# A decoder step on one core: final norm row left unscaled, three operand splits put behind the last head group's post-processing on ScalarE

## The chip, the cores and the metric

The kernel runs on one core of a Trainium2 chip. The metric is the device time of one execution in microseconds (us). The core's engines run side by side, each through its own list of instructions in order: TensorE (PE: matmuls, which write PSUM), VectorE (DVE), ScalarE (ACT), GpSimd (POOL), and SyncE (SP), on whose queue this kernel puts all its transfers. An instruction waits on its engine until what it reads has been written and the buffer that it writes is free; what stands behind it on that engine waits too.

## The reference, cut to what matters

One layer of a hybrid decoder on 2048 prompt tokens and 8 x 8 new tokens: RMSNorm, one input projection, four heads of differential attention, a convolution branch, both gated and concatenated into m, an output projection, residual and a final RMSNorm.

```python
def mix_out(att, conv, g_att, g_conv, w_out):
    m = jnp.concatenate([att * jax.nn.silu(g_att), conv * jax.nn.silu(g_conv)], axis=-1)
    return m @ w_out
...
o = rmsnorm(o, subln_g) * (1.0 - lam_init)
...
yp = yp + mix_out(att, conv, g_att, g_conv, w_out[l])
...
y_prompt = rmsnorm(yp, final_norm_g)
```

`rmsnorm(x, g)` is `x * rsqrt(mean(x*x) + EPS) * g` over rows of D = 1024.

## The kernel before, in words

The first 690 us are the input projections and the convolution; they are not touched. Behind them comes prompt attention, in 13 groups (h, G): head h, 512 query rows G. The order of the groups is h = 0 to 3 with G = 1 to 3 (head 0 from G = 0), and then (1,0), (2,0), (3,0). So (3,3) is the last large group, and three small ones follow it. Each group has four blocks of 128 query rows and two score maps m; each pair (block, m) is a score tile row: PE fills score tiles `S` in PSUM (`s_mm`, two buffers of 1024 columns), DVE takes their row minimum and copies them to SBUF (`s_min`, `pS` or `pL`), ACT makes exponentials with row sums (`exp_row`), POOL two small numbers (`coef`), DVE combines the two maps (`combine`), PE transposes (`pt`), ACT copies the transposes (`at`), and PE multiplies them with the values into `O`.

A group ends with its post-processing: `post1` copies `O` to `osb` and squares it into `o2` on ACT; `post15` adds a small diagonal to `o2` on POOL; `post2` sums the squares over partitions on PE, and takes logarithm and exponential (`rs`) on ACT; POOL multiplies with the gate, and SP writes the result to the scratch `md`.

The output projection works in 8 chunks of 256 tokens, in the order `OC` (2, 3, 4, 5, 6, 7, 0, 1). `out_chunk` loads m from `md` into the one buffer `mf`, and `m_split` makes a rounded high part `mH` (ACT) and the rest `mL` (DVE), so that three matmuls per weight block give the product's precision. `out_tile` does two tiles of 128 tokens, each in two halves of 512 columns: 24 matmuls into `yps`, then DVE adds the residual (`y`), ACT squares with a row sum, POOL takes the power -0.5, DVE scales with the norm row `fnt`, and SP writes the rows out. The weights are split in the same way by `wo_load`; k = 0 and 1 go to buffers of their own, k = 2 to 7 to buffers of the long score rows as these come free. The raw weights (`wor`) lie in the buffers that `mH` and `mL` use later.

The first three chunks are traced at low priority beside the last groups: PE has one PSUM bank for them (pool psM) until attention is over, and three more after that. The small sample attention (`dec_stream`) is interleaved with later chunks.

Nothing orders the engines by hand. The instructions are traced in the program's order with priorities, and a scheduler with a timeline of its own then fixes each engine's list; the list is static, and each engine waits at its head. `tc.issue_after(ins)` makes the instructions traced in its block stand behind `ins` on `ins`'s engine.

Of the kernel before, what the change touches and what calls it, by code (L numbers as in the profile page):

```python
# [1 line left out]

# [9 lines left out]
AF = mybir.ActivationFunctionType  # L12
ALU = mybir.AluOpType
# [5 lines left out]
D = 1024  # L19
# [13 lines left out]
EPS = 1e-5  # L33
# [19 lines left out]
LOW = 3000  # L53
# [3 lines left out]
OC = (2, 3, 4, 5, 6, 7, 0, 1)  # L57
# [17 lines left out]
def hybrid_step(  # L75
# [6 lines left out]
    PE, DVE, ACT, POOL, SP = nc.tensor, nc.vector, nc.scalar, nc.gpsimd, nc.sync  # L82
# [397 lines left out]
    def post1(Gd):  # L480
        osb = op.tile([P, 512], F32, name="osb", tag="osb")
        ACT.activation(osb, Gd["O"], AF.Copy)
        o2 = op.tile([P, 512], F32, name="o2", tag="o2", bufs=1)
        ACT.activation(o2, osb, AF.Square)
        Gd["post"] = osb, o2

    def post15(Gd):
        o2 = Gd["post"][1].rearrange("p (b t) -> p b t", t=P)
# [9 lines left out]
    def post2(Gd):  # L498
        osb, o2 = Gd["post"]
        gate = Gd["gate"]  # L500
        pm = tps()
        PE.matmul(pm, lhsT=onesd, rhs=o2, start=True, stop=True)

        def ev():
            rs = op.tile([P, 512], F32, name="rs", tag="rs", bufs=1)
            ACT.activation(rs, pm, AF.Ln)
            ACT.activation(rs, rs, AF.Exp, scale=-0.5)
            POOL.tensor_tensor(out=osb, in0=osb, in1=gate, op=ALU.mult)
            POOL.tensor_tensor(out=gate, in0=osb, in1=rs, op=ALU.mult)
            SP.dma_start(md[Gd["G"]][:, Gd["h"], :], gate)  # L510
        evac(ev)
# [82 lines left out]
    def tps(side=False):  # L594
        while len(pend) >= TB - 1:
            pend.pop(0)()
        if side:
            return PS["m"].tile([P, 512], F32, name="pt", tag="mt", bufs=PS["n"])
        return psT.tile([P, 512], F32, name="pt", tag="t", bufs=TB)

    def evac(fn):
        pend.append(fn)
# [119 lines left out]
    dk = {}  # L722
# [141 lines left out]
    for n, (h, G) in enumerate(groups):  # L864
        Gd = {"h": h, "G": G, "n": n}
# [34 lines left out]
    def end_unit(U, k):  # L900
        Gd = U["G"]
        h, G = Gd["h"], Gd["G"]
        ts_ = slice(G * 512, (G + 1) * 512)
        first = [U["s"] == 0]
        for fn in pv_items(U):
            def run(fn=fn):
                if first[0]:
                    first[0] = False
                    if (h, G) == (H - 1, 3):
                        pxs.clear()  # L910
                        out_open()
                    Gd["gate"] = op.tile([P, 512], F32, name="gate", tag="gate")
                    SP.dma_start(Gd["gate"], gd[h][:, ts_])
                    Gd["O"] = psO.tile([P, 512], F32, name="O", tag="O")
                U["O"], U["vt"] = Gd["O"], Gd["vt"]
                fn()
                flush()
            queue.append((k + D2, run))
        if U["s"] == 1:
            def p1():  # L920
                if (h, G) == (H - 1, 3):
                    for k in range(2):
                        wo_load(k)
                post1(Gd)
                post15(Gd)
                if h == 0 and G == 3:
                    flags["h0"] = True

            def p2():
                post2(Gd)  # L930
                flush()
                if (h, G) == (H - 1, 3):
                    for k in range(2, KC):
                        wo_load(k)
                    for c in OC[0:NE]:
                        side(out_chunk(c), off=-LOW)
                flags["wide"] = flags.get("wide") and (h, G) != (H - 1, 3)
            queue.append((k + D2, p1))
            queue.append((k + D3, p2))
# [15 lines left out]
    def out_open():  # L955
        nonlocal oy
        px_ctx.close()
        oy = ctx.enter_context(tc.tile_pool(name="oy", bufs=2, side="right", reuse_waits="tile"))
        dk["fnt"] = oy.tile([P, D], F32, name="fnt", tag="fnt", bufs=1)
        SP.dma_start(dk["fnt"], fng.to_broadcast([P, D]))  # L960
        POOL.tensor_scalar(out=dk["fnt"], in0=dk["fnt"], scalar1=float(D) ** 0.5, scalar2=None, op0=ALU.mult)
        for k in range(0, KC, 2):
            r = oy.tile([P, 2, D], F32, name="wor", tag="mH" if k % 4 == 0 else "mL")
            SP.dma_start(r, wout[k * P:(k + 2) * P, :].rearrange("(x p) d -> p x d", p=P))
            wor[k], wor[k + 1] = r[:, 0, :], r[:, 1, :]

    def out_tile(mH, mL, sl, xsrc, dst, nr, last=False):
        y = oy.tile([P, D], F32, name="y", tag="y")
        SP.dma_start(y[0:nr, :], xsrc)
        ss = oy.tile([P, 2], F32, name="yss", tag="yss")  # L970
        for hf in range(2):
            cs = slice(hf * 512, (hf + 1) * 512)
            yb.append(yb.pop(0))
            ps = yb[-1].tile([P, 512], F32, name="yps", tag="mt" if yb[-1] is psM else "y",
                             bufs=1 if yb[-1] is psM else 5 - DM)
            i = 0
            for k in (2, 3, 4, 5, 6, 7, 0, 1):
                for m, x in ((mH, 0), (mL, 0), (mH, 1)):
                    PE.matmul(ps, lhsT=m[:, k, sl], rhs=wo[k][x][:, cs], start=(i == 0), stop=(i == 3 * KC - 1))  # L979
                    i += 1  # L980
            yield
            DVE.tensor_tensor(out=y[0:nr, cs], in0=ps[0:nr, :], in1=y[0:nr, cs], op=ALU.add)  # L982
            jk = oy.tile([P, 512], mybir.dt.bfloat16, name="yjunk", tag="yjunk", bufs=1)
            ACT.activation(jk[0:nr, :], y[0:nr, cs], AF.Square, accum_out=ss[0:nr, hf:hf + 1])
        r = oy.tile([P, 1], F32, name="yr", tag="yr")
        POOL.tensor_scalar(out=r[0:nr, :], in0=ss[0:nr, 0:1], scalar1=ss[0:nr, 1:2], scalar2=D * EPS, op0=ALU.add,
                           op1=ALU.add)
        POOL.tensor_tensor(out=r[0:nr, :], in0=r[0:nr, :], in1=mhalf[0:nr, :], op=ALU.pow)
        for cs in (slice(0, 512), slice(512, D)) if last else (slice(0, D),):
            DVE.scalar_tensor_tensor(out=y[0:nr, cs], in0=y[0:nr, cs], scalar=r[0:nr, :], in1=dk["fnt"][0:nr, cs],  # L990
                                     op0=ALU.mult, op1=ALU.mult)
            SP.dma_start(dst[:, cs], y[0:nr, cs])

    def m_split(mf, n):
        mH = oy.tile([P, KC, 256], F32R, name="mH", tag="mH")
        mL = oy.tile([P, KC, 256], F32R, name="mL", tag="mL")
        ACT.activation(mH[:, :, 0:n], mf[:, :, 0:n], AF.Copy)
        DVE.tensor_tensor(out=mL[:, :, 0:n], in0=mf[:, :, 0:n], in1=mH[:, :, 0:n].bitcast(F32), op=ALU.subtract)
        return mH, mL

    def out_chunk(c, pre=None):
        mf = oy.tile([P, KC, 256], F32, name="mf", tag="mf", bufs=1)
        SP.dma_start(mf, md[c // 2][:, :, c % 2 * 256:c % 2 * 256 + 256])
        mH, mL = m_split(mf, 256)
        sm = pre() if pre else None
        for j in range(2):
            t = 2 * c + j
            yield from out_tile(mH, mL, slice(j * P, (j + 1) * P), xp[t * P:(t + 1) * P, :], yp[t * P:(t + 1) * P, :], P,
                                last=pre is not None and j == 1)
            if sm and j == 0:  # L1010
                yield from out_tile(*sm, slice(0, P), xs, ys, SMP)

    def wo_load(k):
        if k < 2:
            hi, lo = (pp.tile([P, D], F32R, name=f"wo{x}{k}", tag="wo", bufs=4) for x in range(2))
        else:
            tg = "pL1" if k < 4 else "pL0"
            w = pp.tile([P, 2, D], F32R, name=f"wo{k}", tag=tg, bufs=PBUFS[tg])
            hi, lo = w[:, 0, :], w[:, 1, :]
        r = wor[k]  # L1020
        ACT.activation(hi, r, AF.Copy, scale=gsub if k < 4 else 1.0)
        if k < 4:
            DVE.scalar_tensor_tensor(out=lo, in0=r, scalar=gsub, in1=raw(hi), op0=ALU.mult, op1=ALU.subtract)
        else:
            DVE.tensor_tensor(out=lo, in0=r, in1=raw(hi), op=ALU.subtract)
        wo[k] = hi, lo
# [3 lines left out]
    def side(gen, n=10 ** 6, off=0):  # L1030
        with tc.high_priority(offset=off):
            for _ in gen:
                flush()
                n -= 1
                if n <= 0:
                    return False
        return True
# [127 lines left out]
```

## Time and profile before

| what | us |
|---|---|
| median of three runs (lowest, highest) | 1346.87 (1342.31, 1347.28) |
| the profiled execution: its time | 1346.68 |
| its span | 1344.8 |
| mean granted TensorE clock | 0.993 of full |
| matmuls of the output projection | 816, on PE from 1069.7 to 1337.4 |
| PE busy | 1287.8 of the span |

Times within the trace count from the span's start. A matmul's duration includes its pipeline, so that consecutive ones overlap; the distance of their starts is what PE is occupied. In brackets at a row's end stand the idle time of the engine before the instruction, and what ended it.

### The profile page before, as it was taken

The numbers are of one execution on the slowest core, as the hardware profiler recorded it, in microseconds if no ns is written. First come the engines' busy times: TensorE is split into PE (matmuls) and PEld (weight loads), VectorE is DVE, ScalarE is ACT, GpSimd is POOL, SyncE is SP. The second block draws the span as 40 slices with busy tenths as digits, with TensorE's granted clock in tenths as the row PEclk, the third lists the DMA queues.
The fourth block names the chain that finished last, engine by engine and source line by source line (L and its number), as shares of the span: only waits on it lengthen the run. The fifth ranks groups of instructions, "written<-read, shape, count | busy, mean of one in ns | idle before, by whom it ended". The sixth has DMA issues, their size and how long they took to land.

```text
span 1344.8 us, 19974 instructions
## 1 busy us (share of the span) xinstructions
PE 1287.8 (96%) x7552; PEld 1102.4 (82%) x7552; DVE 863.1 (64%) x1215; ACT 516.8 (38%) x949; POOL 249.5 (19%) x353
## 2 busy tenths in 40 slices
PE   6999999999999999999988999999999899999997
PEld 5898998998888888888866888888777677767776
DVE  7623998998999992333127777787778864214332
ACT  6622211211211222323236666656676864212221
POOL 3200200200201100000014233222324345301110
PEclk9999999999999999999989999999999999999999
DMA  8641330330432435333266455454264745558631
GB/s 270 201 132 50 82 119 33 105 112 24 128 112 60 146 141 167 134 119 111 80 139 171 134 152 141 115 150 115 50 147 117 238 111 163 193 189 277 243 126 63
DMA packets 127794, 180.23 MB, mean 134 GB/s; under 512 B 25170, under 2 KB 74578, under 8 KB 127698
## 3 DMA queue, kind: packets, MB, share of 16 engines
q1 hardware_dynamic: 127698, 178.96, 43.9%
q8 instruction: 59, 0.97, 0.3%
q14 instruction: 37, 0.30, 0.1%
HBM read 113.88 MB, written 65.04 MB: 133 GB/s over the span
## 4 chain that ended last, share of the span: by engine, by line
PE 78%; DMA 9%; DVE 4%; ACT 3%; issue 2%; POOL 1%; SPq 1%; DVEq 0%; POOLq 0%; ACTq 0%
PE zps L204 38%; PE yps L979 12%; PE zps L328 7%; PE O L696 6%; PE pt L551 3%; PE S L616 3%; PE pt L678 3%; PE S L617 3%; DMA kt<-kd 2%; DVE pL L661 1%; DMA wr<-in_wz 1%; DVE pL L638 1%; DMA qt<-qd 1%; DMA mf<-md 1%; DMA c<-cd 1%
## 5 line engine op out<-in xcount | busy, mean ns | idle before, releaser
L204 PE MATMUL zps<-hH,wH 128*128 128x512 f32 (+2 forms) x984 | 343.4, 349 | 3.0 <-ACT wH L160 3.0
L204 PE MATMUL zps<-hL,wH 128*128 128x512 f32 (+2 forms) x984 | 343.3, 349 | 0.0
L204 PE MATMUL zps<-hH,wL 128*128 128x512 f32 (+2 forms) x984 | 343.2, 349 | 0.0
L241 DVE SCALAR_TENSOR_TENSOR acc<-u,cst,acc 128x1024 f32<-128x1024 f32 x240 | 313.2, 1333 | 6.9 <-ACT acc L239 4.1
L204 PEld LDWEIGHTS zps<-hH,wH 128*128 128x128 f32 x984 | 185.0, 188 | 25.3 <-ACT wH L160 3.7
L204 PEld LDWEIGHTS zps<-hH,wL 128*128 128x128 f32 x984 | 185.2, 188 | 21.5
L204 PEld LDWEIGHTS zps<-hL,wH 128*128 128x128 f32 x984 | 185.1, 188 | 21.4
L979 PE MATMUL yps<-wo,mH 128*128 128x512 f32 x544 | 176.8, 401 | 0.8 <-DVE y L982 0.8
L616 PE MATMUL S<-kt,qt 128*128 128x512 f32 (+3 forms) x320 | 131.4, 414 | 18.9 <-DMA kt<-kd 4.9
L696 PE MATMUL O<-at,vt 128*128 128x256 f32 (+1 forms) x576 | 141.5, 373 | 1.8 <-ACT at L683 1.6
L979 PEld LDWEIGHTS yps<-wo,mH 128*128 128x128 f32 x544 | 101.7, 188 | 28.2 <-issue 3.2
L649 ACT ACTIVATE pL<-pL,mn 128x1152 f32<-128x1152 f32 (+7 forms) x64 | 104.3, 1630 | 40.9 <-DVE mn L641 40.6
L617 PE MATMUL S<-kt,qt 128*128 128x512 f32 (+3 forms) x320 | 114.9, 369 | 0.0
L696 PEld LDWEIGHTS O<-at,vt 128*128 128x128 f32 x576 | 102.4, 193 | 13.4 <-ACT at L683 2.8
L979 PE MATMUL yps<-wo,mL 128*128 128x512 f32 x272 | 108.7, 400 | 0.0
L683 ACT ACTIVATE at<-pt 128x512 f32<-128x512 f32 (+1 forms) x144 | 79.2, 567 | 55.3 <-PE pt L678 53.9
L638 DVE TENSOR_SCALAR_CACHE_REDUCE pL<-S 128x1024 f32<-128x1024 f32 x64 | 78.1, 1221 | 26.1 <-PE S L617 25.5
L616 PEld LDWEIGHTS S<-kt,qt 128*128 128x128 f32 x320 | 61.3, 192 | 39.0 <-issue 9.6
L661 DVE SCALAR_TENSOR_TENSOR pL<-pL,cf,pL 128x512 f32<-128x512 f32 (+2 forms) x112 | 80.7, 778 | 13.1 <-POOL cf L656 13.0
L641 DVE CUSTOM_DVE_ANT_0 pS<-S,trim 128x768 f32<-128x768 f32 (+7 forms) x64 | 47.2, 754 | 61.8 <-PE S L617 58.7
L982 DVE TENSOR_TENSOR y<-yps,y 128x512 f32<-128x512 f32 (+1 forms) x34 | 23.2, 689 | 90.1 <-PE yps L979 65.8
L655 POOL TENSOR_TENSOR cf<-sm,mone 128x1 f32<-128x1 f32 x64 | 40.2, 628 | 204.8 <-ACT pL L649 110.5
(163 smaller groups left out, 1947.4 us busy)
## 6 DMA issues: line engine op xcount, KB each, us to landing
qt<-qd SPq DMA_DIRECT2D x32, 512.0 KB, 7.2
wr<-in_wz SPq DMA_DIRECT2D x48, 256.0 KB, 3.5
kt<-kd SPq DMA_DIRECT2D x38, 256.0 KB, 5.1
xt<-in_xp SPq DMA_DIRECT2D x16, 512.0 KB, 5.2
mf<-md SPq DMA_DIRECT2D x8, 1024.0 KB, 7.1
y<-in_xp SPq DMA_DIRECT2D x16, 512.0 KB, 3.9
kr<-in_ck SPq DMA_DIRECT2D x32, 256.0 KB, 4.5
vr<-in_cv SPq DMA_DIRECT2D x32, 256.0 KB, 5.4
```

The lines of the kernel that those rows point to most:

```text
L204: PE.matmul(ps[:, 0:n], lhsT=wt[:, ks], rhs=ht[g][:, k, off:off + n], start=(i == 0), stop=(i == 3 * KC - 1))
L241: DVE.scalar_tensor_tensor(out=a, in0=u[:, t:t + HS], scalar=dwwt[:, cg, t:t + 1], in1=a, op0=ALU.mult, op1=ALU.add)
L328: PE.matmul(ps[0:n, 0:256], lhsT=ht[g][:, k, off:off + n], rhs=wt[:, sl], start=(i == 0), stop=(i == 3 * KC - 1))
L616: PE.matmul(ps[:, o:o + n], lhsT=t["mq"][:, m, qs_], rhs=kk, start=True, stop=False)
L617: PE.matmul(ps[:, o:o + n], lhsT=t["mq"][:, 2 + m, qs_], rhs=kk, start=False, stop=True)
L638: DVE.tensor_scalar(out=dst, in0=ps, scalar1=0.0, scalar2=None, op0=ALU.add, op1=ALU.min, accum_out=mn[:, m, 0:1])
L641: DVE.tensor_tensor_reduce(out=dst, in0=ps[:, 0:w], in1=trim[:, 1024 - w:] if diag else trim[:, 0:1].to_broadcast([P, w]), scale=1.0, scal ...
L649: ACT.activation(q, q, AF.Exp, bias=B["mn"][:, m, c:c + 1], scale=-1.0, accum_out=B["sm"][:, m, B["i"] % 4:B["i"] % 4 + 1])
L661: DVE.scalar_tensor_tensor(out=p0, in0=p1, scalar=B["cf"], in1=p0, op0=ALU.mult, op1=ALU.add)
L683: ACT.activation(at[:, 0:n * P], pt[:, 0:n * P], AF.Copy)
L696: PE.matmul(O[:, dst], lhsT=vt[j // 4][:, j % 4, :], rhs=at[:, src], start=(j == 0), stop=part)
L979: PE.matmul(ps, lhsT=m[:, k, sl], rhs=wo[k][x][:, cs], start=(i == 0), stop=(i == 3 * KC - 1))
```

## The change

Three things. The norm row `fnt` is no longer multiplied with the square root of 1024 on POOL; instead the Square of `out_tile` takes a scale of 1024 to the -0.5, and the constant added to the sum is EPS instead of 1024 EPS. The splits of weights k = 0 and 1, which were traced ahead of the post-processing of group (3,3), are traced behind its Square and must stand behind it on ACT. The split `mH` of the first chunk must stand behind that group's exponential on ACT.

```diff
@@ post1
-        ACT.activation(o2, osb, AF.Square)
+        ins = ACT.activation(o2, osb, AF.Square)
         Gd["post"] = osb, o2
+        return ins
@@ post2
-            ACT.activation(rs, rs, AF.Exp, scale=-0.5)
+            Gd["ri"] = ACT.activation(rs, rs, AF.Exp, scale=-0.5)
@@ end_unit
             def p1():
+                ins = post1(Gd)
                 if (h, G) == (H - 1, 3):
-                    for k in range(2):
-                        wo_load(k)
-                post1(Gd)
+                    with tc.issue_after(ins.ins):
+                        for k in range(2):
+                            wo_load(k)
...
-                        side(out_chunk(c), off=-LOW)
+                        side(out_chunk(c, tail=Gd["ri"].ins if c == OC[0] else None), off=-LOW)
@@ out_open
         SP.dma_start(dk["fnt"], fng.to_broadcast([P, D]))
-        POOL.tensor_scalar(out=dk["fnt"], in0=dk["fnt"], scalar1=float(D) ** 0.5, scalar2=None, op0=ALU.mult)
@@ out_tile
-            ACT.activation(jk[0:nr, :], y[0:nr, cs], AF.Square, accum_out=ss[0:nr, hf:hf + 1])
+            ACT.activation(jk[0:nr, :], y[0:nr, cs], AF.Square, scale=float(D) ** -0.5, accum_out=ss[0:nr, hf:hf + 1])
...
-        POOL.tensor_scalar(out=r[0:nr, :], in0=ss[0:nr, 0:1], scalar1=ss[0:nr, 1:2], scalar2=D * EPS, op0=ALU.add,
+        POOL.tensor_scalar(out=r[0:nr, :], in0=ss[0:nr, 0:1], scalar1=ss[0:nr, 1:2], scalar2=EPS, op0=ALU.add,
@@ out_chunk
-    def out_chunk(c, pre=None):
+    def out_chunk(c, pre=None, tail=None):
...
-        mH, mL = m_split(mf, 256)
+        with tc.issue_after(tail) if tail else nullcontext():
+            mH, mL = m_split(mf, 256)
```

The scheduler answers with another order from about 1041 us of the old trace on; ahead of that, PE's list is the same. Line numbers of the kernel after are higher by one or two.

ACT at the end of group (3,3), before. The first row copies its last transposes; osb and o_10210 are the copy and the Square of its output, mH is the split of the second chunk, rs the logarithm; pS rows are exponentials of the small groups:

```order
L683 ACTIVATE at<-pt 128x384
L1021 ACTIVATE wo_10248<-wor 128x1024
L649 ACTIVATE pS_10696,sm<-pS_10696,mn 128x512
L482 ACTIVATE osb<-O 128x512
L484 ACTIVATE o_10210<-osb 128x512
L649 ACTIVATE pS_10718,sm<-pS_10718,mn 128x128
L997 ACTIVATE mH<-mf 128x2048
L984 ACTIVATE yjunk,yss<-y 128x512
L506 ACTIVATE rs<-pt 128x512
L683 ACTIVATE at<-pt 128x384
```

The same place after. o_10201 is the Square; wo_10203 and wo_10207 are weights 0 and 1, and mH is here the first chunk's split:

```order
L1023 ACTIVATE wo_10247<-wor 128x1024
L482 ACTIVATE osb<-O 128x512
L484 ACTIVATE o_10201<-osb 128x512
L1023 ACTIVATE wo_10203<-wor,gsub 128x1024
L1023 ACTIVATE wo_10207<-wor,gsub 128x1024
L507 ACTIVATE rs<-pt 128x512
L684 ACTIVATE at<-pt 128x384
L508 ACTIVATE rs<-rs 128x512
L998 ACTIVATE mH<-mf 128x2048
L650 ACTIVATE pS_10707,sm<-pS_10707,mn 128x128
L650 ACTIVATE pS_10724,sm<-pS_10724,mn 128x256
```

Both weight splits and the first mixed split have come to this place. The splits of weights 0 and 1 stood some 40 rows ahead of the copy before, and the first chunk's mH stood in the middle of the long exponentials.

PE at the same place, before. The rows O<-at,vt_9542 end group (3,3); yps are matmuls of the first chunk:

```order
L979 MATMUL yps<-wo_10242,mL 128x512
L979 MATMUL yps<-wo_10242,mH 128x512
L979 MATMUL yps<-wo_10245,mH 128x512
L979 MATMUL yps<-wo_10245,mL 128x512
L696 MATMUL O<-at,vt_9542 128x256
L696 MATMUL O<-at,vt_9542 128x128
L979 MATMUL yps<-wo_10245,mH 128x512
L979 MATMUL yps<-wo_10248,mH 128x512
L979 MATMUL yps<-wo_10248,mL 128x512
L616 MATMUL S<-kt_10079,qt 128x128 x2
L617 MATMUL S<-kt_10079,qt 128x128 x2
L979 MATMUL yps<-wo_10248,mH 128x512
```

And after. L503 is the sum over squares of (3,3), pS_10099 to pS_10669 are score rows of group (1,0):

```order
L697 MATMUL O<-at,vt_9542 128x256
L697 MATMUL O<-at,vt_9542 128x128
L503 MATMUL pt<-o_10201,onesd 128x512
L679 MATMUL pt<-ident,pS_10099 128x128
L679 MATMUL pt<-ident,pS_10119 128x128 x2
L679 MATMUL pt<-ident,pS_10221 128x128
L679 MATMUL pt<-ident,pS_10669 128x128
L679 MATMUL pt<-ident,pS_10221 128x128
L679 MATMUL pt<-ident,pS_10669 128x128
L697 MATMUL O<-at,vt_9780 128x256
L697 MATMUL O<-at,vt_9780 128x128
L679 MATMUL pt<-ident,pS_10221 128x128
```

The yps rows have gone from here: the first of them now stands six rows further down, behind score tiles of group (2,0). Before, 24 of them stood ahead of this group's sum over squares, and 93, 144 and 192 ahead of those of (1,0), (2,0) and (3,0). After, it is 0, 24, 92 and 144.

DVE at the second chunk, before. The first row is the residual add that frees the first half's PSUM bank, and mL is the low part of the second chunk:

```order
L982 TENSOR_TENSOR y<-yps,y 128x512
L641 ISA pS_10708,mn<-S,trim 128x128
L641 ISA mn 128x1
L641 ISA pS_10725,mn<-S,trim 128x256
L641 ISA mn 128x1
L998 TENSOR_TENSOR mL<-mf,mH 128x2048
L661 SCALAR_TENSOR_TENSOR pS_10708<-pS_10718,cf,pS_10708 128x128
L641 ISA pS_10748,mn<-S,trim 128x256
L641 ISA mn 128x1
L982 TENSOR_TENSOR y<-yps,y 128x512
```

And after; pS rows with mn are minima of group (2,0):

```order
L662 SCALAR_TENSOR_TENSOR pS_10724<-pS_10747,cf,pS_10724 128x256
L642 ISA pS_10781,mn<-S,trim 128x384
L642 ISA mn 128x1
L642 ISA pS_10792,mn<-S,trim 128x512
L642 ISA mn 128x1
L999 TENSOR_TENSOR mL<-mf,mH 128x2048
L983 TENSOR_TENSOR y<-yps,y 128x512
L662 SCALAR_TENSOR_TENSOR pS_10764<-pS_10781,cf,pS_10764 128x384
L642 ISA pS_10810,mn<-S,trim 128x512
L642 ISA mn 128x1
```

The first half's add has gone from ahead of the second chunk's low part to behind it. On SP's queue the load of the third small group's keys, which stood behind the first rows written out, now stands ahead of them, behind the load of the second chunk.

## Rows read from the trace of the kernel before

**Rows 1.** From the page: the span, and PE's busy time with its share and number of instructions.

```profile
span 1344.8 us, 19974 instructions
...
PE 1287.8 (96%) x7552; PEld 1102.4 (82%) x7552; DVE 863.1 (64%) x1215; ACT 516.8 (38%) x949; POOL 249.5 (19%) x353
```

**Rows 2.** The view of stretches, PE alone: the stretch in us, its width, PE's busy time (number of instructions), PE's granted clock, share of the DMA engines, GB/s.

```profile
1050.00:1060.00 10.00, 7.82 (x32) 1.00 0.75 271
1060.00:1070.00 10.00, 8.99 (x48) 1.00 0.37 94
1070.00:1080.00 10.00, 8.78 (x53) 1.00 0.48 118
1080.00:1092.10 12.10, 12.10 (x66) 1.00 0.41 102
1092.10:1106.00 13.90, 12.73 (x62) 1.00 0.53 122
1106.00:1119.90 13.90, 13.12 (x57) 1.00 0.67 207
1119.90:1122.40 2.50, 0.19 (x1) 1.00 0.92 212
1122.40:1126.20 3.80, 3.79 (x11) 0.55 0.00 0
...
1166.00:1220.00 54.00, 51.60 (x378) 1.00 0.66 220
```

**Rows 3.** PE's instructions in order of time: start, duration, engine, line, operation, what is written from what, count, and in brackets the idle time before and what ended it.

```profile
1059.35 1.12 PE L502 MATMUL pt<-o,onesd 128*128 128x512 f32 x2 [1.90 <-POOL o L496]
...
1088.06 0.58 PE L979 MATMUL yps<-wo,mL 128*128 128x512 f32 x1
...
1091.27 0.81 PE L696 MATMUL O<-at,vt 128*128 128x256 f32 x4
...
1103.28 0.44 PE L678 MATMUL pt<-ident,pS 128*128 128x128 f32 x2 [0.83 <-ACT rs L506]
...
1115.16 0.51 PE L979 MATMUL yps<-wo,mH 128*128 128x512 f32 x1 [0.78 <-DVE y L982]
...
1122.41 0.45 PE L616 MATMUL S<-kt,qt 128*128 128x128 f32 x1 [2.32 <-DMA kt<-kd]
```

**Rows 4.** ACT's instructions in order of time, the same columns.

```profile
1044.45 1.14 ACT L1021 ACTIVATE wo<-wor,gsub 128x1024 fp32r<-128x1024 f32 x1
...
1056.89 0.62 ACT L484 ACTIVATE o<-osb 128x512 f32<-128x512 f32 x1
1057.41 1.89 ACT L997 ACTIVATE mH<-mf 128x2048 fp32r<-128x2048 f32 x1
...
1092.12 0.60 ACT L482 ACTIVATE osb<-O 128x512 f32<-128x512 f32 x1 [2.54 <-PE O L696]
1092.75 0.63 ACT L484 ACTIVATE o<-osb 128x512 f32<-128x512 f32 x1
...
1100.22 1.92 ACT L997 ACTIVATE mH<-mf 128x2048 fp32r<-128x2048 f32 x1 [6.29 <-DMA mf<-md]
...
1102.65 0.57 ACT L506 ACTIVATE rs<-pt 128x512 f32<-128x512 f32 x1
1103.13 0.48 ACT L683 ACTIVATE at<-pt 128x384 f32<-128x384 f32 x1
...
1104.38 0.62 ACT L507 ACTIVATE rs<-rs 128x512 f32<-128x512 f32 x1
```

**Rows 5.** POOL's instructions in order of time.

```profile
1041.85 2.78 POOL L961 TENSOR_SCALAR fnt<-fnt 128x1024 f32<-128x1024 f32 x1 [4.50 <-PE pt L678]
1044.64 0.57 POOL L655 TENSOR_TENSOR cf<-sm,mone 128x1 f32<-128x1 f32 x1
...
1057.58 1.71 POOL L496 TENSOR_TENSOR o<-o,dgs 128x512 f32<-128x512 f32 x1 [2.08 <-ACT o L484]
...
1093.47 1.28 POOL L496 TENSOR_TENSOR o<-o,dgs 128x512 f32<-128x512 f32 x1 [2.46 <-ACT o L484]
```

**Rows 6.** DVE's instructions in order of time.

```profile
1047.95 1.28 DVE L1023 SCALAR_TENSOR_TENSOR wo<-wor,gsub,wo 128x1024 fp32r<-128x1024 f32 x1
...
1056.09 3.49 DVE L661 SCALAR_TENSOR_TENSOR pL<-pL,cf,pL 128x512 f32<-128x512 f32 x4
...
1094.88 0.69 DVE L982 TENSOR_TENSOR y<-yps,y 128x512 f32<-128x512 f32 x1 [1.48 <-PE yps L979]
...
1102.17 2.29 DVE L998 TENSOR_TENSOR mL<-mf,mH 128x2048 fp32r<-128x2048 f32 x1 [5.44 <-ACT mH L997]
```

**Rows 7.** SP's queue in order of time: two loads of mixed chunks, with the time from the start of the first one's issue to the end of the second one's.

```profile
1089.02 16.01 SPq L1003 DMA_DIRECT2D mf<-md  x2
```

**Rows 8.** From the view of the tile mf: its loads' times from issue to landing, the shortest being the one of 128 KB and the others of 1 MB.

```profile
DMA to landing us min/median/max: 3.5/6.9/11.2
```

**Rows 9.** The chain of waits in order of time: start, us, what, count.

```profile
1158.79 0.86 PE pt L502 x2
...
1303.81 33.61 PE yps L979 x144
```

**Rows 10.** Groups of ACT's instructions by line from 1041 to 1166 us: line, operation, shapes, count, busy us, mean ns, idle before.

```profile
L649 ACT ACTIVATE pS<-pS,mn 128x128 f32<-128x128 f32 (+3 forms) x24 | 13.3, 558 | 15.6 <-DVE mn L641 15.4
...
L1021 ACT ACTIVATE wo<-wor 128x1024 fp32r<-128x1024 f32 x4 | 4.2, 1051 | 0.8 <-PE pt L678 0.8
```

More of the change, by code (lines that the diff above doesn't have):

```diff
@@ L1 @@
-from contextlib import ExitStack
+from contextlib import ExitStack, nullcontext
 import concourse.bass as bass
```

## The prediction

> **What bounds the kernel now.** I read the page first. TensorE (PE) is busy for 96% of the span [rows 1], so the time is PE's work plus the places where PE stands still or runs at its lower clock. The change removes no matmul, so its effect is the change in those two. The order of instructions is the same up to about 1041 us, and so I read PE's busy time by stretches from there [rows 2]. In each row the reader takes the width of the stretch less PE's busy time. That leaves 2.18, 1.01 and 1.22 us in the three stretches from 1050 to 1080, nothing from 1080 to 1092.1, 1.17 from 1092.1 to 1106, 0.78 to 1119.9, and 2.31 to 1122.4. The stretch behind it has a granted clock of 0.55 (the 1.2 GHz level, after a stretch in which PE did almost nothing); at full clock its 3.80 us would have taken 0.45 x 3.80 = 1.71 us less. The sum from 1050 to 1126.2 is 8.67 + 1.71 = 10.4 us. Another 2.4 us lies between 1166 and 1220; the rest is PE working.
>
> Then the order of PE in time shows what stood before PE when it resumed [rows 3]: POOL's add to the squared output (1.90 us), ACT's logarithm (0.83), the add that frees the one PSUM bank of the output projection (0.78), a key load (2.32). The row at 1088.06 starts the output projection's matmuls in the middle of the last attention groups. They are the filler: PE does them while short attention chains run on ACT, POOL and DVE. One takes 33.61 / 144 = 0.233 us [rows 9].
>
> The profiled execution took 1346.68 us with a span of 1344.8; the median of the three runs is 1346.87. I add changes to 1346.7.
>
> **The change, part by part.** *The norm row left unscaled* removes one POOL instruction of 2.78 us. POOL had been idle for 4.50 us before it, and its next instruction, a coefficient, began at 1044.64 [rows 5], when the exponential that it needs had ended only just before 1044.45, where the next ACT row starts [rows 4]. At most 0.2 us was lost there; from above it could give back 2.78. The factor moves into the scale of a Square and into a constant: no instruction more. I take 0.
>
> *The splits of weights 0 and 1* leave the stretch of the long exponentials: two ACT instructions of 1.14 us [rows 4] and two DVE ones of 1.28 [rows 6]. *The first mixed split* (1.89 us on ACT at 1057.41) leaves it too, and in the new order the Square of group (3,2) stands directly behind its copy, where before a long exponential stood between (the Square starts at 1056.89, and PE's wait for the add behind it ended at 1059.35). The 4.4 us that PE stood still from 1050 to 1080 are what this can return. Since DVE's two splits (2.6 us) stood in its chain there, but DVE's minimum over each score tile still releases PE's next tile, I take 2.5 of 4.4. The ends are 0 and 4.4.
>
> *What the splits' new place costs.* Call T the end of the last attention product of group (3,3) on PE. Before, the copy on ACT followed it at once (1091.27 + 0.81 = 1092.08, copy at 1092.12, [rows 3, 4]), and PE had filler matmuls until the logarithm's input was ready. In the new order no filler stands there: PE's first projection matmul comes behind the group's sum over squares, the next group's transposes and its score tiles. So PE waits for the whole chain:
> - ACT: the exponential of 128 (0.56 with its short reading behind) and the split of weight 7 (1.05, [rows 10]) stand before the copy, which starts at T+1.1; copy and Square, 0.60 and 0.63, end at T+2.3.
> - POOL's add 1.28 [rows 5], then PE's sum over squares 0.86 [rows 9]: T+4.6 with the hand-overs. The splits of weights 0 and 1 (2.3 us) run on ACT beside it and end at T+4.4, so they cost little themselves.
> - ACT: logarithm, copy of the transposes, exponential, mixed split: 0.57 + 0.48 + 0.62 + 1.92 with overlap [rows 4] gives T+8.0. DVE's low part, 2.29 [rows 6]: T+10.4.
> PE has 4.1 us of work of its own up to there: the sum over squares 0.86, ten transposes and six products of attention (2.4), two score tiles (0.6) and one projection matmul. It stands still 6.3 us. Its first wait, until T+3.7, is longer than the 2.3 us behind which the clock fell before [rows 2], so the 0.86 us instruction doubles and all behind it comes 0.9 later. I take 7.2 us, low part ready at T+11.3, against 1.17 before: +6.0. The ends: 3.7 less 1.17, or +2.5, if only the wait up to the sum over squares remains, and +8 if ACT's other exponentials come late.
>
> Here the Trainium skill bears on one row. POOL's add took 1.71 us at 1057.58, while DVE combined two score rows from SBUF (3.49 us for four), and 1.28 at 1093.47 [rows 5, 6]. The page "SBUF — State Buffer", section "Who interferes with whom", says that a DVE instruction with two SBUF inputs contends with a GpSimd instruction that reads SBUF; the splits' low parts have two such inputs, and DVE has four of them around T. By this rule the add takes the 1.71 us again, and the sum below would be 0.4 us higher; by the undisturbed row it stays. The trace agrees with the rule at 1057.58. I keep 1.28, because weight 7's low part should be over when the add starts.
>
> *The next mixed chunk.* Its load cannot be issued before DVE has the first low part, as before (the load's issue was held from 1089.02 on, [rows 7]). On ACT its split stands in front of the second group's exponentials and logarithm; on DVE its low part now stands in front of the add that frees the only PSUM bank, where before the add came first (1094.88 against 1102.17, [rows 6]). The load issued at T+11.3 lands 6.9 us later, the median [rows 8]: T+18.2; split 1.92, low part 2.29, add 0.69: T+23.1. PE meanwhile has 23 projection matmuls (5.4), one sum over squares, three transposes and three score tiles (2.5): to T+19.2. It waits about 4.0, of which two attention products take 0.4: 3.6 us, and then the clock falls once more, 1.7. That is 5.3 us. Before, the same part held the bank's wait 0.78, the key load's 2.31 and 1.71 of low clock, 4.8 in all; the key load is now issued before the chunk's output traffic and has 6 us of matmuls over it. So +0.5. The ends: a load of 3.5 us, as the short one took, leaves 0.2 of waiting and no fall of the clock (-4.6); one of 11.2, as this very load had, adds 4.3 (+4.8).
>
> *Behind that*, 48 filler matmuls (11.2 us) move from before to behind the last attention groups, where PE has nothing else to wait for. The 2.4 us of waits from 1166 to 1220 stay, give or take 2.
>
> Sum: -2.5 + 6.0 + 0.5 = +4.0, or 1350.7 us.
>
> **The rivals.**
> - *The load behind the split decides* (slower). If the second mixed chunk lands after 11 us rather than 7, ACT's exponentials, the bank and PE all wait for it: +4.3 more, 1355.0, and 1357.5 if the early stretch gives nothing back. It decides from a landing of about 9.6 us. For it: its 11.2 us in this trace, with PE's order now hanging on it. Against: then two key loads and a query load stood just in front of it, which now come earlier. 0.22.
> - *The early gain wins* (faster). All 4.4 us of waiting from 1050 to 1080 go, the first chain costs only its lower end (+2.5), and the load is hidden (-4.6): 1346.7 - 6.5 = 1340.2. For it: ACT and DVE lose 4 to 5 us of work where both are nearly full. Against: PE's order holds no filler at T, and no row shows a way round the Square, add and logarithm. 0.15.
> - *Nothing but a trade.* The waits move from one place to another and the sum stays near 10.4 us: 1346.7, give or take 1.5. That is also the case in which PE's moved filler is missed nowhere. For it: the waits of before were no smaller a list. 0.18.
> - My forecast, 0.45, between 1347.5 and 1354.
>
> **How the numbers follow.** About 0.5% (6.7 us) is what a measurement of this kernel tells from no change: faster means below 1340.0, slower above 1353.4. Slower: most of the first rival (0.20) and the top of the forecast (0.06), 0.26. Faster: half of the second rival and a little for what I have not seen, 0.11. The rest, 0.63, is within 0.5%. The range goes from 1341.5, which leaves out half of the second rival, to 1358, the end of the first. The forecast's own range is 1347.5 to 1354.
>
> **What would show it.** Right: from 1050 to 1080 PE stands still some 2 us instead of 4.4; no projection matmul before group (3,3)'s sum over squares, and a wait of 3 to 4 us before it ended by POOL; a wait of PE for ACT or DVE before the second half of the first projection tile, with the chunk's load the last thing in front of it; a granted clock near half behind one of them; no wait for a key load. Wrong: fewer than 3 us of waiting in the 12 us behind T, which would speak for the second rival, or a long wait elsewhere, above all among the sample's loads behind 1166, which I have taken as unchanged.

## The result, and the profile after

The changed kernel takes 1366.61 us (median of 4 runs, 1357.85 to 1367.88), and the kernel before 1347.07 beside it: a ratio of 1.0131, 95% interval 1.0103 to 1.0158. The change makes the kernel slower by about 1.3%. The forecast was 1350.7 with a range up to 1358.0, and it gave "slower" a chance of 0.26: it was wrong in size and in its likeliest case. The profiled execution took 1367.88 us. All traces here are of single executions, and a kernel's executions differ: the four of the changed kernel span 10 us.

The page's first lines (the span; PE's busy time, share and instructions):

```profile
span 1366.1 us, 19969 instructions
...
PE 1295.2 (95%) x7552; PEld 1108.1 (81%) x7552; DVE 866.3 (63%) x1215; ACT 517.8 (38%) x949; POOL 249.4 (18%) x352
```

The matmuls are the same 7552 as in [rows 1]; the span is 21.3 us longer, and PE's busy time rose by only 7.4, which is in the main matmuls at a lower clock (6.8 us, counted from the granted clocks below). The rest is PE standing still. The view of stretches says where (PE alone, columns as in [rows 2]; T, the end of the last attention product of group (3,3), is now at 1093.4):

```profile
1050.00:1060.00 10.00, 7.75 (x37) 1.00 0.91 336
1060.00:1070.00 10.00, 9.40 (x48) 1.00 0.29 82
1070.00:1080.00 10.00, 7.58 (x45) 1.00 0.64 130
1080.00:1093.40 13.40, 10.80 (x63) 1.00 0.57 138
1093.40:1107.00 13.60, 10.79 (x39) 0.75 0.17 53
1107.00:1117.50 10.50, 8.28 (x34) 0.93 0.60 174
1117.50:1124.00 6.50, 6.50 (x31) 0.85 0.60 189
1124.00:1162.00 38.00, 37.11 (x168) 1.00 0.33 102
1162.00:1170.00 8.00, 2.54 (x34) 0.82 0.87 302
1170.00:1178.00 8.00, 5.55 (x14) 0.54 0.56 207
1178.00:1186.00 8.00, 7.22 (x43) 1.00 0.46 133
...
1220.00:1260.00 40.00, 39.22 (x312) 1.00 0.70 228
1260.00:1270.00 10.00, 7.59 (x58) 0.83 0.70 255
```

In each row the loss is the width less the busy time, and the busy time times what is missing of the granted clock. By the prediction's own terms, before and after:

| stretch of the program | before | after | difference | predicted |
|---|---|---|---|---|
| early, 1050 to T | 4.4 | 7.9 | +3.5 | -2.5 |
| first chain behind T (after: 1093.4 to 1107) | 1.2 | 5.5 | +4.3 | +6.0 |
| second mixed chunk (after: 1107 to 1124) | 4.8 | 3.8 | -1.0 | +0.5 |
| all behind that, to 1270 | 2.5 | 17.0 | +14.5 | 0 |
| sum | 12.9 | 34.2 | +21.3 | +4.0 |

The sum is the whole difference of the spans. The two terms behind T came out within 2 us of their forecast; the early gain has the wrong sign; and two thirds of the loss lie in the part that was taken as unchanged. What PE waited for (PE in order of time, in brackets the idle time and what ended it):

```profile
1060.46 0.50 PE L617 MATMUL S<-kt,qt 128*128 128x512 f32 x1 [1.46 <-DVE mn L642]
...
1072.19 0.30 PE L617 MATMUL S<-kt,qt 128*128 128x128 f32 x1 [2.33 <-DMA kt<-kd]
...
1089.89 0.41 PE L617 MATMUL S<-kt,qt 128*128 128x128 f32 x2 [1.69 <-DMA kt<-kd]
...
1096.08 2.08 PE L503 MATMUL pt<-o,onesd 128*128 128x512 f32 x2 [2.70 <-POOL o L497]
...
1114.87 0.92 PE L697 MATMUL O<-at,vt 128*128 128x256 f32 x4 [2.22 <-ACT at L684]
...
1165.45 0.64 PE L764 MATMUL dS<-kr,Qx 128*32 128x256 f32 x8 [2.63 <-DMA kr<-in_ck]
1168.60 1.08 PE L764 MATMUL dS<-kr,Qx 128*32 128x256 f32 x8 [2.51 <-DMA kr<-in_ck]
1172.45 0.79 PE L980 MATMUL yps<-wo,mH 128*128 128x512 f32 x1 [2.77 <-DVE y L983]
```

The two key loads are new; the wait of 2.70 us for POOL's add and the one of 2.22 us are the ones foreseen. The last three lines are the largest item: the sample attention's first score products `dS` wait for cache pages (`kr`), and the next half tile of the projection waits for the bank that DVE's add of the input rows (`y`) frees. A smaller item, 3.7 us from 1260 to 1270, is four waits of the sample's products with the values (`dO`) for value pages, the longest 1.83 us, and the low clock with them; what made these pages late was not followed up. The chain of waits (start, us, what) tells why the rows came late:

```profile
1144.89 2.33 POOL yr L987
...
1149.22 5.83 DMA out_yp<-y
...
1159.68 1.93 DMA qk<-qsd
...
1162.92 1.27 POOL gate L510
...
1165.11 6.57 DMA y<-in_xp
...
1172.45 7.19 PE yps L980 x20
```

Everything goes through one queue. On SP, in order:

```profile
1147.07 0.55 SPq L1004 DMA_DIRECT2D mf<-md  x1
1149.22 0.34 SPq L993 DMA_DIRECT2D out_yp<-y  x1
1149.61 5.76 SPq L730 DMA_DIRECT2D smt<-in_smask  x8
...
1161.85 1.94 SPq L759 DMA_DIRECT2D kr<-in_ck  x4
1164.21 0.33 SPq L511 DMA_DIRECT2D md<-gate  x1
1164.64 0.38 SPq L993 DMA_DIRECT2D out_yp<-y  x1
1165.11 0.45 SPq L970 DMA_DIRECT2D y<-in_xp  x1
```

A chunk's load (`mf`) stands at the head until DVE has the low part; the output store behind it waits for POOL and DVE; the sample's 21 set-up loads follow and take 12 us to issue; the row load on which PE's next half tile depends is last, behind four page loads, the store of an attention result and that of an output tile. Its buffer was free when the output store of 1149.22 had landed, at 1155.05, so it went out 10 us later than it could. Before, this row load was issued at 1140.41 and the next one at 1149.67, both ahead of the set-up loads (1150.86). Behind such a stretch the clock falls too: 0.54 from 1170 to 1178, so mostly its lower level, after 8 us with 2.54 us of work.

### The profile page after: what moved, and what is told of

Read it like the earlier page. It is cut to its first block, busy times and chain, and to the rows that moved or that the text cites. A ratio compares the mean times of both kernels' runs of the same rounds, so it can differ in the third digit from the quotient of the medians.

```text
span 1366.1 us, 19969 instructions
## 1 busy us (share of the span) xinstructions
PE 1295.2 (95%) x7552; PEld 1108.1 (81%) x7552; DVE 866.3 (63%) x1215; ACT 517.8 (38%) x949; POOL 249.4 (18%) x352
## 5 line engine op out<-in xcount | busy, mean ns | idle before, releaser
L980 PE MATMUL yps<-wo,mH 128*128 128x512 f32 x544 | 180.8, 407 | 4.7 <-DVE y L983 4.7
L662 DVE SCALAR_TENSOR_TENSOR pL<-pL,cf,pL 128x512 f32<-128x512 f32 (+2 forms) x112 | 80.7, 778 | 10.7 <-POOL cf L657 10.5
L642 DVE CUSTOM_DVE_ANT_0 pS<-S,trim 128x384 f32<-128x384 f32 (+7 forms) x64 | 47.2, 754 | 58.2 <-PE S L618 57.8
```

Of the source, the lines that this page charges most:

```text
L642: DVE.tensor_tensor_reduce(out=dst, in0=ps[:, 0:w], in1=trim[:, 1024 - w:] if diag else trim[:, 0:1].to_broadcast([P, w]), scale=1.0, scal ...
L662: DVE.scalar_tensor_tensor(out=p0, in0=p1, scalar=B["cf"], in1=p0, op0=ALU.mult, op1=ALU.add)
```

## The experiments

Two theories stood at the start. The *sample theory*: the largest loss is only where the scheduler put the sample's loads and its first products. The *filler theory*: holding the first mixed split back takes the projection matmuls away from where PE needs them, and everything else follows. In the diffs below "after" is the changed kernel.

**Run 1: the norm row alone.** Before, with the first part of the change (the constant EPS goes with it):

```diff
-        POOL.tensor_scalar(out=dk["fnt"], in0=dk["fnt"], scalar1=float(D) ** 0.5, ...
...
-            ACT.activation(jk[0:nr, :], y[0:nr, cs], AF.Square, accum_out=...
+            ACT.activation(jk[0:nr, :], y[0:nr, cs], AF.Square, scale=float(D) ** -0.5, accum_out=...
...
```

> The kernel before with the first part of the change alone: the norm row is left unscaled, its factor goes into the scale of the Square and the constant; all other instructions stand in the order of before. The theory that the order carries the whole result expects no difference: 1344 to 1349 us, ratio 0.998 to 1.002. The rival, that taking the 2.78 us off POOL brings something by itself, expects it faster by up to 2.8 us; a loss here (over 1350) would say that the scaled Square costs time.

Measured: 1345.93 us against 1345.57, ratio 0.9998 (0.998 to 1.0015). Within 0.2% this part does nothing, and the scaled Square costs nothing.

**Run 2: no hold on the first mixed split.** After, with

```diff
-        with tc.issue_after(tail) if tail else nullcontext():
-            mH, mL = m_split(mf, 256)
+        mH, mL = m_split(mf, 256)
```

> The changed kernel without its third part: the first mixed split is free again, the splits of weights 0 and 1 stay behind the Square. PE's order at the start of the sample attention is like that of the changed kernel: 24 projection matmuls behind the last group's sum over squares, then two score products in a row from pages that are still being loaded. The theory that the sample's start is the largest loss (12 us of the 21) expects some 10 to 12 us of waiting and low clock among the sample's page loads here too, and 1354 to 1362 us. The rival, that holding back the first mixed split is what costs (no filler matmuls under the last long group, and all that follows), expects it within 4 us of before, 1343 to 1351.

Measured: 1341.55 us, ratio 0.9977 (0.9957 to 0.9997); measured again as run 9 below. One line takes 21 us (by the ratios) to 25 (by the medians) from the changed kernel. The sample theory's forecast failed, and the time is a little under the filler theory's 1343 too. PE's order has the 24 matmuls and the 16 score products in a row here too, but the loss at the sample's start is 0.9 us. SP's queue and PE in this run:

```profile
1135.47 0.33 SPq L970 DMA_DIRECT2D y<-in_xp  x1
1140.21 3.58 SPq L730 DMA_DIRECT2D smt<-in_smask  x8
1150.28 1.99 SPq L759 DMA_DIRECT2D kr<-in_ck  x4
```

```profile
1154.97 0.61 PE L764 MATMUL dS<-kr,Qx 128*32 128x256 f32 x8
1156.13 0.64 PE L764 MATMUL dS<-kr,Qx 128*32 128x256 f32 x8 [0.54 <-DMA kr<-in_ck]
```

The row load is issued in front of the set-up loads, and the pages are issued 4.7 us before PE asks for them; in the changed kernel PE came to the products 1.0 us after that issue (1165.45 less the wait of 2.63 is 1162.82, against 1161.85). So PE's order alone is not the cause; runs 4 to 6 test it together with SP's.

**Run 3: no move of weights 0 and 1.** After, with the two splits again in front of the copy:

```diff
-                ins = post1(Gd)
                 if (h, G) == (H - 1, 3):
-                    with tc.issue_after(ins.ins):
-                        for k in range(2):
-                            wo_load(k)
+                    for k in range(2):
+                        wo_load(k)
+                post1(Gd)
```

> The changed kernel without its second part: the splits of weights 0 and 1 stand in front of the copy as before, the first mixed split waits for the last long group's exponential. PE again has 24 projection matmuls and then two score products in a row at the sample's start, and the first projection matmul comes behind the short group's transposes. Both theories expect it slow. The sample theory: 10 to 12 us at the sample's start and 4 to 6 us in the chain behind the last long group, 1360 to 1368. The rival that holding back the mixed split costs everything: the whole loss, 1364 to 1370, of which little has to lie at the sample's page loads.

Measured: 1357.39 us, ratio 1.0081 (1.0052 to 1.011). Both theories missed it, with 1360 to 1368 and 1364 to 1370: the losses lie where the sample theory put them (10.5 us at the sample's start, the chain 4 us above before; table below), but the early part stays small without the weight move. By the medians the hold costs 11.5 us without the weight move (1357.39 less run 1's 1345.93) and 25 with it (1366.61 less 1341.55); by the ratios, which compare each kernel with the one before measured beside it, 11 and 21. The weight move gains 3 to 4 us without the hold and costs 7 to 9 with it. The two parts are not a sum.

**Run 4: the sample's first products later.** After, with

```diff
-            heads(L["S"][:, i * 256:(i + 1) * 256], 256, lambda h: L["Qx"][:, h, a, :],
+            with tc.issue_after(halves[8].ins) if j == 0 else nullcontext():
+                heads(L["S"][:, i * 256:(i + 1) * 256], 256, lambda h: L["Qx"][:, h, a, :],
```

(`halves` holds the last matmul of each half tile of the projection).

> The changed kernel with one more order: the sample's first score products on PE stand 48 projection matmuls (11.2 us) later; up to there the order of all engines is that of the changed kernel. The sample theory expects the waits for pages (2.63 + 2.83 us) and most of the low clock behind them (2.9 us) gone, and the 2.45 us for the input rows too if they only came late with the pages: 8 to 12 us faster than the changed kernel, 1354 to 1359. The rival, that the loss is set by the late projection work as a whole and only shows at the sample's loads, expects the waits to reappear at the input rows or at the next pages, and 1363 to 1368.

Measured: 1362.61 us, ratio 1.0125 (1.0092 to 1.0158). The time is just under the rival's 1363. The pages no longer make PE wait; the rows do, as the rival said:

```profile
1168.32 0.80 PE L981 MATMUL yps<-wo,mH 128*128 128x512 f32 x1 [9.12 <-DVE y L985]
```

**Run 5: the row load first, and run 6: both.** After, with the set-up loads behind the fourth row load (run 5), and with the edit of run 4 as well (run 6):

```diff
-                dec_open()
+                with tc.issue_after(yl[3].ins):
+                    dec_open()
...
-        SP.dma_start(y[0:nr, :], xsrc)
+        yl.append(SP.dma_start(y[0:nr, :], xsrc))
```

> The changed kernel, with the sample's set-up loads queued behind the fourth input-row load of the projection on SP (in the changed kernel that row load stands behind 25 of the sample's loads, though its buffer is free at about 1151 us). The theory that SP's queue makes the loss behind 1160 (the rows come at 1171.7, and PE, which has only the projection and pages to do, stands still) expects the 9 to 11 us of waiting and low clock from 1162 to 1178 nearly gone: 1353 to 1359. The rival, that the pages (whose loads are issued later still) are the bound there and the row load only one of two waits, expects the waits to stay at the page loads: 1361 to 1367.

> Both orders on the changed kernel: the sample's set-up loads behind the fourth input-row load, and its first score products behind 48 projection matmuls. The theory of SP's queue expects the same as with the row load first alone, or up to 2 us less: 1352 to 1358, and no wait over 1 us for pages or rows up to 1185. The rival of two separate waits expects the gain only here: 1352 to 1358 while the row load first alone stays over 1361.

Measured: 1361.06 us (ratio 1.0107, 1.0083 to 1.0131) and 1354.31 (1.0055, 1.002 to 1.0091). By the medians each alone gives 4 to 6 us and both give 12; by the ratios 1, 3 and 10. The intervals of run 4 and run 5 overlap that of the changed kernel (1.0103 to 1.0158), so neither gain is shown by itself; that of run 6 does not, and its gain is. This is what the rival of two separate waits said, though run 5's 1361.06 lies at the edge of its range. The expectation of run 5 put the row load's buffer free at about 1151; by the trace it was 1155, and in runs 5 and 6 the load goes out 5.8 and 6.0 us after the store that frees it. With the rows early, run 5 still waits 1.82 us for pages, and run 4 waited for rows. In run 6 nothing waits there for over 0.8 us (SP, then PE):

```profile
1153.22 0.33 SPq L972 DMA_DIRECT2D y<-in_xp  x1
1153.65 3.88 SPq L730 DMA_DIRECT2D smt<-in_smask  x8
1163.98 1.95 SPq L759 DMA_DIRECT2D kr<-in_ck  x4
```

```profile
1168.44 0.50 PE L982 MATMUL yps<-wo,mH 128*128 128x512 f32 x1 [0.78 <-DVE y L986]
1174.23 1.07 PE L764 MATMUL dS<-kr,Qx 128*32 128x256 f32 x16
```

So 10 to 12 of the 18 to 20 us come from the order of SP's and PE's lists at the sample's start, and can be had back with the hold in place. About 7 remain (1354.31 against 1347.28).

**Run 7: the hold at the Square.** After, with the mixed split behind `post1`'s Square (kept as `Gd["sq"]`) and not behind the exponential:

```diff
-                        side(out_chunk(c, tail=Gd["ri"].ins if c == OC[0] else None), off=-LOW)
+                        side(out_chunk(c, tail=Gd["sq"].ins if c == OC[0] else None), off=-LOW)
```

> The changed kernel with the first mixed split held only behind the Square of the last long group, not behind its exponential. PE's order changes little and the order behind 1124 not at all. If what the late split costs grows with its delay, the second mixed chunk's load is issued 3 to 5 us earlier, and the wait of 2.22 us in front of the attention product and the low clock behind it (1.6 us) go: 1361 to 1364. If the loss is set by the place of the projection in the order, and not by the delay of this split, the time stays: 1365 to 1368.

Measured: 1363.4 us, ratio 1.013 (1.0104 to 1.0156). The median is 3 us less, inside the forecast of a cost that grows with the delay, but the ratio is that of the changed kernel (1.0131): no difference is shown, and this run does not decide between its two theories. The wait of 2.22 us for ACT went, as expected, but the next group's wait for POOL's add became 4.20 us: PE came to it earlier, and POOL was late by a coefficient that took 2.06 us beside DVE's next low part (more on that at the end). The wait moved more than it went.

**Run 8: an early split, but no filler at T.** Run 2, with the projection matmuls of the first chunk queued on PE behind the sum over squares of group (3,3):

```diff
-                    PE.matmul(ps, lhsT=m[:, k, sl], rhs=wo[k][x][:, cs], ...
+                    with tc.issue_after(hold) if hold else nullcontext():
+                        PE.matmul(ps, lhsT=m[:, k, sl], rhs=wo[k][x][:, cs], ...
```

> The changed kernel without the hold on the first mixed split (as in the run without the mixed gate); instead PE's first projection matmuls are queued behind the last long group's sum over squares. So the split is as early as in that run, and PE stands without filler as in the changed kernel. In SP's order the sample's set-up loads again stand in front of an input-row load. The theory that PE's missing filler is what costs, wherever the split stands, expects a wait of 2.5 us or more for POOL's add in front of the sum over squares, with low clock behind it, and more waits at the sample's start: 1350 to 1362. The rival, that the late split itself costs (ACT, DVE and the second chunk's load behind it), expects it within 4 us of the run without the gate: 1338 to 1346.

Measured: 1355.45 us, ratio 1.007 (1.0043 to 1.0096), 12 us more than run 9 and 14 more than run 2, with the split itself free (it ran on ACT at 1079.3, ahead of T):

```profile
1091.83 2.08 PE L503 MATMUL pt<-o,onesd 128*128 128x512 f32 x2 [2.70 <-POOL o L497]
```

This is the changed kernel's wait to the hundredth, with the same doubled duration. SP's order also came out like the changed kernel's (set-up loads at 1138.12, row load at 1152.15). So the filler theory holds for the wait at T: it comes when PE has no matmul to do there, however early the split is. But only 3 us of the loss over run 2 lie in this chain (5.3 against 2.3, table below), and the changed kernel loses 4.4 more there, with the late split. Most of the rest, 6.4 us at the sample's start and 3.6 behind it, is the scheduler's answer to one constraint on PE.

**Run 9: run 2 again, with more executions.**

> The run without the mixed gate once more, with more rounds, to tell it from the kernel before. If the two first parts of the change gain by themselves: 1339 to 1344, ratio 0.995 to 0.999 with an interval below 1. If its first measurement was a lucky mix of runs: 1344 to 1348, and an interval that holds 1.

Measured: 1343.04 us against 1346.64, ratio 0.9979 (0.9966 to 0.9992). The first two parts of the change without the third are 0.2% faster than the kernel before.

The losses of all profiles, counted as in the table above from stretches of about 4 us and aligned at the sum over squares of group (3,3), S: the early part is S-45 to S-5, the chain and the second chunk S-5 to S+31, the sample's start S+31 to S+91, the rest to S+230. The boundaries differ a little from those of the table. The losses belong to the profiled execution, whose time stands beside the median; in runs 1 to 8 it is the fastest of its kernel or the next to it.

| kernel | early | chain, second chunk | sample's start | rest | sum | profiled us | median us |
|---|---|---|---|---|---|---|---|
| before | 4.4 | 5.8 | 0.1 | 2.4 | 12.7 | 1346.68 | 1347.07 |
| 1 norm row alone | 4.9 | 4.9 | 0.1 | 1.3 | 11.2 | 1341.05 | 1345.93 |
| 2 no hold | 6.7 | 2.3 | 0.9 | 0.8 | 10.7 | 1338.76 | 1341.55 |
| 9 the same again | 7.7 | 2.4 | 1.6 | 0.8 | 12.5 | 1346.75 | 1343.04 |
| 3 no weight move | 5.3 | 9.9 | 10.5 | 1.0 | 26.7 | 1355.17 | 1357.39 |
| after | 7.9 | 9.7 | 12.6 | 4.7 | 34.9 | 1367.88 | 1366.61 |
| 4 sample later | 7.9 | 7.1 | 13.5 | 0.9 | 29.4 | 1361.43 | 1362.61 |
| 5 rows first | 8.4 | 8.0 | 5.9 | 2.0 | 24.3 | 1356.83 | 1361.06 |
| 6 both | 8.4 | 9.8 | 2.5 | 1.5 | 22.2 | 1352.87 | 1354.31 |
| 7 hold at the Square | 7.2 | 9.6 | 11.1 | 1.6 | 29.5 | 1360.20 | 1363.40 |
| 8 no filler at T | 7.0 | 5.3 | 7.3 | 4.4 | 24.0 | 1353.11 | 1355.45 |

The reader is to see three things. The early part is 6.7 or more wherever weights 0 and 1 are moved, and 5.3 or less where they are not: its loss belongs to the second part of the change. The chain is 2.3 in runs 2 and 9, with filler and an early split, 5.3 without filler, 9.7 with a late split as well (4.9 and 5.8 in run 1 and before, where a key load is waited for). The sample's start goes with SP's order: it is 7.3 to 13.5 in the five kernels in which the set-up loads stand in front of the fourth row load, and 5.9 or less in the others.

## Why the prediction was wrong

- *The norm row, 0.* Right (run 1).
- *The early stretch, -2.5: failed, it is +3.5.* The step that the waits from 1050 to 1080 "are what this can return" counted only the waits that were there, and they did not return. POOL's add went from 1.90 to 1.25 us, but a wait of 1.46 for DVE's minimum stands where the longest of this kind was 0.83: without the key loads, the waits up to T are 3.8 us, before 3.9. The two waits for key loads, 2.33 and 1.69, came on top, and by the trace they come from PE's own order. SP issues the first of these loads when PE has read the old keys for the last time (before, then after: the end of PE's score product, and the issue 0.03 us behind it; SP's waits name this product in both):

```profile
1062.18 0.40 PE L617 MATMUL S<-kt,qt 128*128 128x512 f32 x1
1062.61 1.24 SPq L710 DMA_DIRECT2D kt<-kd  x2
...
1065.48 0.39 PE L618 MATMUL S<-kt,qt 128*128 128x512 f32 x1
1065.90 1.24 SPq L711 DMA_DIRECT2D kt<-kd  x2
```

  PE then came to the new keys 8.4 us behind the issue before (1071.0), and 4.0 us after (1069.9). For the second load it was 6.2 us (1086.38 to 1092.62) and 3.9 (1084.30 to 1088.20); before, 16 projection matmuls stood just in front of these tiles. In run 2, with the same 4.0 us, PE waited 1.71 at the first of these tiles for DVE's minimum, so the load alone need not be worth the whole 2.33.
- *The first chain, +6.0: 4.3 measured; the wait at T was right, its sizes were not.* No filler stood at T, PE waited for POOL, and the clock fell. But PE stood still 2.8 us where 6.3 were counted, and the lower clock cost 2.7 where 0.9 was; that the sum is near is in part luck. The wait was 2.70 and not 3.7, since the copy followed the last product at once (the exponential and weight 7's split ended before T). The second wait, for the low part, did not come: PE had twelve products of attention to do up to there and not six, and did its work at a mean clock of 0.75. The low part was ready at T+11.1, forecast T+11.3. POOL's add took 1.27 us: the undisturbed row was the right one to take.
- *The second mixed chunk, +0.5: -1.0.* The load took 6.2 us from issue to use by ACT, forecast 6.9; the wait was 2.22 where 3.6 was forecast, and the clock cost 1.6, forecast 1.7. No key load was waited for in this stretch.
- *"The 2.4 us of waits from 1166 to 1220 stay, give or take 2": failed, and this is the miss.* It is the line that the prediction itself named as what would make it wrong. The step moved 48 matmuls "from before to behind the last attention groups, where PE has nothing else to wait for". But PE got through attention 3 us earlier (the last sum over squares started at 1155.65, before at 1158.62), SP's list had been fixed by the scheduler's own timeline, and PE reached rows and pages that SP had barely issued. The step spoke of PE alone; the loads' order on SP, with the row load behind the set-up loads, is where 12.6 us of loss sit (0.1 before); runs 5 and 6 gave most of it back by that order and PE's.
- *The rivals.* "The load behind the split decides" had the right sign but not the mechanism: that load took 6.2 us, not 11. The other two are out.

What stays open: where the 0.2% of runs 2 and 9 comes from; their losses (10.7 and 12.5) can't be told from those of before and run 1 (12.7 and 11.2). The 7 us that run 6 keeps lie by the table for the most part in the early part and the chain, some 4 us each above before; no run took them away with the hold in place. The value pages at 1260 were not looked into either.

## What to carry to other kernels

A change of one engine's order is a change of all lists where a scheduler fixes them: before costing the waits it removes, read the DMA queue of before and after for every load that an engine will need behind the change, and ask what stands in front of it. Filler work for the busiest engine was worth most where it had nothing else to do beside a chain; delaying the step that releases it cost more here than the step freed elsewhere. A load that waits for the busiest engine to free its buffer has only the work between that engine's last read and its next to land in: count this distance in the new order. Where two loads are late in one place, removing one can show little; remove both.

## What the runs showed of the hardware

A POOL instruction on one number per partition that starts beside DVE's low part ends only with it. In the changed kernel, POOL (the last row is the same instruction as the one above it, with nothing beside it):

```profile
1113.33 2.06 POOL L656 TENSOR_TENSOR cf<-sm,mone 128x1 f32<-128x1 f32 x1 [3.60 <-ACT pS L650]
...
1143.52 1.37 POOL L495 TENSOR_TENSOR dgs<-ident,ss 128x512 f32<-128x512 f32 x1
1144.88 2.34 POOL L987 TENSOR_SCALAR yr<-yss 128x1 f32<-128x1 f32 x1
...
1157.40 0.30 POOL L987 TENSOR_SCALAR yr<-yss 128x1 f32<-128x1 f32 x1 [3.04 <-ACT yjunk L985]
```

and DVE:

```profile
1112.69 2.29 DVE L999 TENSOR_TENSOR mL<-mf,mH 128x2048 fp32r<-128x2048 f32 x1 [1.89 <-ACT mH L998]
...
1143.92 3.12 DVE L999 TENSOR_TENSOR mL<-mf,mH 128x2048 fp32r<-128x2048 f32 x1
```

One number per partition costs 0.30 us alone and 2.34 beside a low part, and it ends 0.18 us behind it (1147.22 and 1147.04). The coefficient of 2.06 us ends 0.41 behind its low part. DVE's low part can take longer too, 3.12 against 2.29 in [rows 6]; but there POOL's product of 128x512 was still running when it started, and beside the coefficient it took its usual 2.29. So in these cases the instruction that came second waited. This agrees with the Trainium skill, page "SBUF — State Buffer", section "Who interferes with whom", that DVE and GpSimd share a pair of ports and that the share is an exclusive lock. The 2.34 us stand in the chain of waits above, 2 us of it in front of SP's store and the loads behind it; what they cost by themselves was not tried. The prediction had weighed the rule for POOL's add at T, where it did not strike, and not for the small instructions, where it did.

The lower clock does not always set in at the same place behind the same wait. Behind 2.69 or 2.70 us for POOL's add, the two matmuls of the sum over squares took 2.08 us in the changed kernel and in runs 6 and 8, 1.54 and 1.49 in runs 4 and 7, and in run 5 1.12, as at full clock:

```profile
1093.99 1.12 PE L503 MATMUL pt<-o,onesd 128*128 128x512 f32 x2 [2.69 <-POOL o L497]
```
